# Five kept places for split weights from the output projection to the plain FFN tiles, and the down projection's group additions on VectorE

## The chip, the cores and the metric

One core of a Trainium2 chip runs one launch of the kernel. The metric is the device time of the launch in microseconds (us); the kernel before is given as the median of three runs. Engines: PE is TensorE, DVE is VectorE, ACT is ScalarE, POOL is GpSimd, SP is SyncE, whose queue issues the weight DMAs.

## The reference

One decoder layer of width 2048 on 512 tokens in float32: token mixing, cross-attention into 256 memory tokens, and a SwiGLU feed-forward of width 5632. The parts that matter here are the end of the cross-attention and the feed-forward:

```python
for l in range(DEPTH):
    ...
    y = memory_cross_attention(h, mem_n, w_xq[l], w_xkv[l], w_xo[l])   # ends in o @ wo, 512 x 2048
    x = x + rms_norm(y, ln_x_post[l])
    h = rms_norm(x, ln_ffn_pre[l])
    y = (jax.nn.silu(h @ w_gate[l]) * (h @ w_up[l])) @ w_down[l]
    x = x + rms_norm(y, ln_ffn_post[l])
```

## The kernel before

Every matrix product is done in three matmuls of a reduced-precision type: a float32 value is split into a high part, a cast on ScalarE (L96), and a low part, the difference, on VectorE (L97), and `mm3` (L112 to L114) issues high x high, high x low and low x high. A weight tile therefore costs a DMA into a raw buffer, a cast and a subtraction before TensorE can use it. The raw buffers are a ring of four (`wraw`), the parts a ring of three (`whi`, `wlo`). The 512 tokens stand in the columns and are worked in two halves of 256 (`HALVES`) from the cross-attention's output projection to the plain FFN tiles. The order of instructions on each engine is made by a scheduler from the dependences and the order of the program; `high_priority(AHEAD)` brings a weight's DMA, cast and subtraction forward.

The output projection `wo(j, t, stat)` runs over 8 weight tiles j of `w_xo` for half t = 0, then t = 1. `net.kept` puts the last three tiles of the first half at the front of the second half, since their parts still stand in the ring; the other five are loaded and split again. In the first half the last attention head is done between the tiles. Then come the inputs of the FFN, `ffn_input(k, t, stat)`, 16 tiles of each half: a DMA of the residual (L641), two VectorE operations (L643, L646), a DMA out (L647), a split (L99 on ScalarE, L100 on VectorE) and a square on ScalarE (L201), whose sums are taken by GpSimd (L203) and by small matmuls against a vector of ones (L213). The first half's inputs and `plain(0)`, the four plain tiles of the FFN (16 weight tiles of 512 KB of `w_gu`) follow; then the second half's inputs (`second()`) and `plain(1)`, which again begins with the three weight tiles that are kept.

The other 40 FFN tiles and most of the down projection are done by a Strassen scheme (`strassen`). For a group it loads 6 or 8 weight tiles of 256 KB, makes three combinations of each (L948 and L949 on VectorE, L950 on GpSimd), casts and subtracts 128x896 (L96, L97), and does 21 matmuls into PSUM banks psO, psG, psS, psT. At the end of a group ScalarE copies one bank and VectorE adds the results into `e` (L963 to L966). In the FFN `swiglu` follows, two VectorE operations of 128x512 (L877, L879) and a silu between them (L878). In the down projection there are two rounds s of 8 groups; after each group GpSimd adds `e` into two output tiles, 128x512 each, 32 additions in all:

```python
for k, o in ((j, 0), (j + hp, 5)):
    nc.gpsimd.tensor_tensor(ys[k], ys[k], e[:, o * 256:(o + 2) * 256], op=ALU.add)   # L1063
```

Of the kernel before, what the change touches and what calls it, by code (L numbers as in the profile page):

```python
# [33 lines left out]
class Net:  # L34
    def __init__(self, ctx, tc, a):
        self.tc, self.nc, self.a = tc, tc.nc, a
        nc = self.nc
        self.rings = {}
        self.const = ctx.enter_context(tc.tile_pool(name="const", bufs=1))
        self.wp = ctx.enter_context(tc.tile_pool(name="wp", bufs=1))  # L40
        self.tp = ctx.enter_context(tc.tile_pool(name="tp", bufs=2))
        self.ps = ctx.enter_context(tc.tile_pool(name="ps", bufs=1, space=PSUM))
        self.dr = ctx.enter_context(tc.tile_pool(name="dr", bufs=1, space=DRAM))
        c = self.const
        right = ctx.enter_context(tc.tile_pool(name="rpad", bufs=1, side="right"))
        nc.vector.memset(right.tile([P, 8], F32, name="rpad"), 0.0)
        self.gains = c.tile([P, len(GAINS), KD], F32, name="gains")
        nc.gpsimd.dma_start(self.gains, a["gains"])
        self.ident = c.tile([P, P], F32, name="ident")
        nc.gpsimd.dma_start(self.ident, a["c_ident"])  # L50
        self.ones = c.tile([P, P], F32, name="ones")
        nc.vector.memset(self.ones, -0.375)
        self.oneD = c.tile([P, 1], F32, name="oneD")
        nc.vector.memset(self.oneD, 1.0 / D)

    def ring(self, name, dtype, n):
        if name not in self.rings:
            self.rings[name] = [[self.wp.tile([P, 1024], dtype, name=f"{name}{i}") for i in range(n)], 0]
        r = self.rings[name]
        r[1] += 1  # L60
        return r[0][(r[1] - 1) % n]

    def kept(self, order):

        return [*order[-3:], *order[:-3]]

    def wtiles(self):
        return self.ring("wraw", F32, 4), self.ring("whi", FR, 3), self.ring("wlo", FR, 3)

# [32 lines left out]
    def weight(self, src, into=None):  # L102
        n = src.shape[1]
        raw, hi, lo = self.wtiles() if into is None else (self.ring("wraw", F32, 4), *into)
        with self.tc.high_priority(AHEAD):
# [544 lines left out]
def sublayer2(net, mctx, ms):  # L650
# [164 lines left out]

    held, last_j = {}, range(KD // 2)[-3:]

    def wo(j, t, stat):
        hi, lo = held[j] = held.pop(j) if t and j in last_j else net.weight(a["w_xo"][j])
        for jj in range(2):  # L820
# [15 lines left out]
    for j in range(KD // 2):  # L836
        if j in (0, 2, 4):
            next(last)
        wo(j, 0, st0)
    k3ctx.close()  # L840
    net.rstd(st0, rb[:, HALVES[0]])
    st1, stx = MeanSq(net, ka, nc.gpsimd, 256, "sy1"), MeanSq(net, ka, nc.gpsimd, 256, "sx0")
    for j in net.kept(range(KD // 2)):
        wo(j, 1, st1)
# [16 lines left out]

    return xctx, xs, x0, yctx, ys, rbf, rf, x2T, second, close

# [5 lines left out]

def ffn(net, xctx, xs, xt0, yctx, ys, rb, rf, x2T, second, close):  # L870
    tc, nc, a = net.tc, net.nc, net.a
# [12 lines left out]
    def plain(t):  # L884
# [5 lines left out]
        parts = [[q for q in order if q[1] == f] for f in range(NPLAIN)]  # L890
        for j, f in order:
            ps, first, last = banks[f], (j, f) == parts[f][0], (j, f) == parts[f][-1]
            if (j, f) in held:
                hi, lo = held.pop((j, f))
            else:
                u, hi, lo = [v.rearrange("p (j b c) -> p j b c", b=4, c=P) for v in net.wtiles()]
                with tc.high_priority(AHEAD):
                    nc.sync.dma_start(u, a["w_gu"][f, j:j + 2].rearrange("j p b c -> p j b c"))
                    net.split(hi, lo, u)
            if not t and (j, f) in order[-3:]:  # L900
                held[j, f] = hi, lo
# [143 lines left out]
    for s in range(2):  # L1045
# [11 lines left out]
        for j in range(hp):  # L1057
# [4 lines left out]
            for k, o in ((j, 0), (j + hp, 5)):  # L1062
                nc.gpsimd.tensor_tensor(ys[k], ys[k], e[:, o * 256:(o + 2) * 256], op=ALU.add)  # L1063
        late = net.last(nc.vector, nc.scalar)
# [230 lines left out]
```

## Time and profile before

| | us |
|---|---|
| median of three runs | 2799.49 (2798.63 to 2800.45) |
| the profiled execution | 2799.45 |
| its span | 2797.7 |
| TensorE busy in it | 2741.7 (98%) |
| VectorE busy | 2011.7 (72%) |
| ScalarE busy | 1252.1 (45%) |
| GpSimd busy | 612.8 (22%) |
| mean TensorE clock granted | 0.996 of full |

The profile comes from one execution. A row of a timeline gives the start within the span, the length, the engine, the source line of the kernel and the tiles written and read; in brackets stands how long the engine had been idle and what ended that. The length of an instruction overlaps a little with the next one's on its engine, so the distance from start to start is the shorter and better price. A row of waits gives the idle time of an engine by the instruction that it waited for. Matmuls of 128x256 follow each other at 0.12 us.

### The profile page before, as it was taken

To read this page: it belongs to the slowest core of one execution; us is meant where nothing else is said; L and a number is where in the kernel's file an instruction comes from. 1 tells how busy PE (TensorE), PEld (TensorE's weight loads), DVE (VectorE), ACT (ScalarE), POOL (GpSimd) and SP (SyncE) were. 2 spreads that over 40 slices of the span, in tenths; PEclk is the share of its full clock that TensorE was granted. 3 is DMA by queue.
4 is the path that set the end of the run, shared out by engine and by line. 5 is a ranking of instruction groups with operands and counts; after the bars stand their busy time and mean duration, and the time that the engine had idled before them with its cause. 6 is when DMAs were issued, how large, how long until landed. Compare 5 with 4: busy or idle time off the path is not lost.

```text
span 2797.7 us, 48879 instructions
## 1 busy us (share of the span) xinstructions
PE 2741.7 (98%) x18384; PEld 2517.8 (90%) x18384; DVE 2011.7 (72%) x3752; ACT 1252.1 (45%) x2061; POOL 612.8 (22%) x715
## 2 busy tenths in 40 slices
PE   9999999999999999999999999999999999999998
PEld 7788887888878889999989999999999999989996
DVE  5655656565645445777798888888988888899756
ACT  4333545454533235654764444444444444343353
POOL 0000000000000000010333444444224223525303
PEclk9999999999999999999999999999999999999999
DMA  6434332333336456763564444444444453444474
GB/s 186 117 101 131 99 96 78 97 97 109 96 105 200 146 154 213 240 214 121 166 203 128 121 118 120 119 121 120 122 115 125 117 170 105 119 136 106 150 247 165
DMA packets 168493, 384.16 MB, mean 137 GB/s; under 512 B 19312, under 2 KB 39840, under 8 KB 168128
## 3 DMA queue, kind: packets, MB, share of 16 engines
q1 hardware_dynamic: 158816, 352.39, 42.1%
q0 software_dynamic: 8864, 27.60, 3.0%
q8 instruction: 144, 2.36, 0.4%
q10 hardware_dynamic: 576, 1.05, 0.1%
q14 instruction: 93, 0.76, 0.1%
HBM read 343.32 MB, written 37.64 MB: 136 GB/s over the span
## 4 chain that ended last, share of the span: by engine, by line
PE 78%; DVE 12%; DMA 6%; issue 2%; ACT 1%; POOL 0%; DVEq 0%; SPq 0%; POOLq 0%; ACTq 0%
PE psG L112 15%; PE psG L114 15%; PE psG L113 15%; DVE wlo L97 5%; PE psS L112 4%; PE psS L113 4%; PE psS L114 4%; PE psT L112 3%; PE psT L114 3%; PE psT L113 3%; DMA wraw<-in_w_dst_dram 3%; DMA wraw<-in_w_gu_dram 2%; PE psO L114 2%; PE psO L112 2%; PE psO L113 2%
## 5 line engine op out<-in xcount | busy, mean ns | idle before, releaser
L96 ACT CAST whi<-wraw 128x896 fp32r<-128x896 f32 (+2 forms) x773 | 758.3, 984 | 1064.1 <-PE psT L114 340.8
L97 DVE TENSOR_TENSOR wlo<-wraw,whi 128x896 fp32r<-128x896 f32 (+2 forms) x773 | 907.4, 1175 | 263.8 <-ACT whi L96 261.0
L950 POOL TENSOR_TENSOR wraw<-wraw 128x128 f32<-128x128 f32 x416 | 415.6, 1001 | 676.1 <-DVE wraw L949 546.9
L112 PE MATMUL psG<-xh,whi 128*128 128x512 f32 (+1 forms) x1072 | 401.0, 374 | 1.6 <-ACT whi L96 1.5
L114 PE MATMUL psG<-xh,wlo 128*128 128x512 f32 (+1 forms) x1072 | 400.1, 373 | 0.8 <-DVE wlo L97 0.8
L113 PE MATMUL psG<-xl,whi 128*128 128x512 f32 (+1 forms) x1072 | 399.7, 373 | 0.0
L112 PEld LDWEIGHTS psG<-xh,whi 128*128 128x128 f32 x1072 | 203.1, 189 | 35.6 <-ACT whi L96 2.9
L114 PEld LDWEIGHTS psG<-xh,wlo 128*128 128x128 f32 x1072 | 202.4, 189 | 33.9 <-DVE wlo L97 1.0
L113 PEld LDWEIGHTS psG<-xl,whi 128*128 128x128 f32 x1072 | 202.8, 189 | 32.5
L948 DVE TENSOR_TENSOR wraw<-wraw 128x128 f32<-128x128 f32 x416 | 137.8, 331 | 103.2 <-DMA wraw<-in_w_gu_dram 67.3
L949 DVE TENSOR_TENSOR wraw<-wraw 128x256 f32<-128x256 f32 x416 | 185.6, 447 | 6.8
L112 PE MATMUL psT<-th,whi 128*128 128x256 f32 x640 | 179.4, 280 | 0.0
L113 PE MATMUL psT<-tl,whi 128*128 128x256 f32 x640 | 178.8, 279 | 0.0
L114 PE MATMUL psT<-th,wlo 128*128 128x256 f32 x640 | 178.7, 279 | 0.0
L114 PE MATMUL psG<-x,wlo 128*128 128x256 f32 (+1 forms) x544 | 158.1, 291 | 3.3 <-DVE wlo L97 3.3
L112 PE MATMUL psG<-x,whi 128*128 128x256 f32 (+1 forms) x544 | 156.8, 288 | 1.5 <-ACT z L764 1.5
L113 PE MATMUL psG<-x,whi 128*128 128x256 f32 (+1 forms) x544 | 157.5, 290 | 0.0
L112 PE MATMUL psG<-mh,whi 128*128 128x256 f32 x512 | 143.4, 281 | 1.1 <-ACT y L630 1.1
L113 PE MATMUL psG<-ml,whi 128*128 128x256 f32 x512 | 143.1, 280 | 0.0
L114 PE MATMUL psG<-mh,wlo 128*128 128x256 f32 x512 | 142.7, 281 | 0.0
L112 PE MATMUL psS<-xh,whi 128*128 128x256 f32 x480 | 134.8, 281 | 1.4 <-ACT xh L99 1.4
L113 PE MATMUL psS<-xl,whi 128*128 128x256 f32 x480 | 135.0, 282 | 0.9 <-DVE xl L100 0.9
(482 smaller groups left out, 7297.2 us busy)
## 6 DMA issues: line engine op xcount, KB each, us to landing
wraw<-in_w_gu_dram SPq DMA_DIRECT2D x320, 256.0 KB, 2.7
wraw<-in_w_z_dram SPq DMA_DIRECT2D x64, 512.0 KB, 3.8
wraw<-in_w_mix_dram SPq DMA_DIRECT2D x64, 512.0 KB, 4.5
wraw<-in_w_down_dram SPq DMA_DIRECT2D x61, 512.0 KB, 5.3
wraw<-in_w_dst_dram SPq DMA_DIRECT2D x96, 256.0 KB, 2.7
wraw<-in_w_gu_dram SPq DMA_DIRECT2D x29, 512.0 KB, 3.7
wraw<-in_w_qk_dram SPq DMA_DIRECT2D x24, 512.0 KB, 3.6
actT<-zs POOLq DMA_DIRECT2D x40, 256.0 KB, 2.3
```

The source lines that it names most:

```text
L96: nc.scalar.copy(hi, x)
L97: nc.vector.tensor_tensor(lo, x, hi.bitcast(F32), op=ALU.subtract)
L112: mm(ps, lh, rh, start=start, stop=False)
L113: mm(ps, lh, rl, start=False, stop=False)
L114: mm(ps, ll, rh, start=False, stop=stop)
L948: nc.vector.tensor_tensor(u[:, 4], u[:, 0], u[:, 3], op=ALU.add)
L949: nc.vector.tensor_tensor(u[:, 5:7], u[:, 0:5:4], u[:, 1:2].broadcast_to([P, 2, P]), op=ALU.subtract)
L950: nc.gpsimd.tensor_tensor(u[:, 7], u[:, 2], u[:, 6], op=ALU.subtract)
```

## The change

Two edits. The ring of parts gets two more places (`kh`, `kl`) for a time: they are made in the space of the pool `k3`, which holds the tiles of the attention heads, when that is closed after the fifth tile of the first half of `wo`, and taken out again at the middle of `plain(1)`. `kept` goes by the number of places that the ring has, so that `wo` and `plain` reuse five tiles in their second half, not three. And the two additions at the end of a down projection's group move from GpSimd to VectorE.

```diff
+    def more(self, slots):
+        self.parts[:0] = slots
+
+    def fewer(self, slots):
+        self.parts[:] = [s for s in self.parts if s not in slots]
 
     def kept(self, order):
-        return [*order[-3:], *order[:-3]]
+        n = len(self.parts)
+        return [*order[-n:], *order[:-n]]
...
-    held, last_j = {}, range(KD // 2)[-3:]
+    held = {}
 
     def wo(j, t, stat):
-        hi, lo = held[j] = held.pop(j) if t and j in last_j else net.weight(a["w_xo"][j])
+        if t and j in held:
+            hi, lo = held.pop(j)
+        else:
+            hi, lo = net.weight(a["w_xo"][j])
+            if not t:
+                held[j] = hi, lo
...
         wo(j, 0, st0)
-    k3ctx.close()
+        if j == 4:
+            k3ctx.close()
+            kw = k2ctx.enter_context(tc.tile_pool(name="kw", bufs=1, side="right"))
+            wide = net.slots(kw, FR, 2, "kh", "kl")
+            net.more(wide)
...
-    for j in net.kept(range(KD // 2)):
+    order = net.kept(range(KD // 2))
+    for j in order[len(net.parts):]:
+        held.pop(j)
+    for j in order:
         wo(j, 1, st1)
...
-        for j, f in order:
+        for i, (j, f) in enumerate(order):
+            if t and i == len(order) // 2:
+                net.fewer(wide)
...
-            if not t and (j, f) in order[-3:]:
+            if not t and (j, f) in order[-len(net.parts):]:
                 held[j, f] = hi, lo
...
             for k, o in ((j, 0), (j + hp, 5)):
-                nc.gpsimd.tensor_tensor(ys[k], ys[k], e[:, o * 256:(o + 2) * 256], op=ALU.add)
+                nc.vector.tensor_tensor(ys[k], ys[k], e[:, o * 256:(o + 2) * 256], op=ALU.add)
```

The rest of the diff gives the rings another form with the same places. The lines of the changed kernel are numbered 10 higher around the splits and 24 higher from the FFN on. In its order VectorE has 32 additions more and 4 splits less, ScalarE 4 casts less, GpSimd 32 additions less, SyncE 4 DMAs of 512 KB less (11 of `w_xo`, not 13; 27 of `w_gu`, not 29), and TensorE the same number of instructions.

VectorE at the end of a group of the down projection's first round, before (L965 and L966 are the last writes of `e`; the L97 behind them is the next group's second weight tile):

```order
L965 TENSOR_TENSOR e_23901<-psT_23736,e_23901 128x512
L966 TENSOR_TENSOR e_23901<-psT_23736,e_23901 128x256
L948 TENSOR_TENSOR wraw1_184<-wraw1_184 128x128
L97 TENSOR_TENSOR wlo0_190<-wraw3_186,whi0_187 128x896
L949 TENSOR_TENSOR wraw1_184<-wraw1_184 128x256
L948 TENSOR_TENSOR wraw2_185<-wraw2_185 128x128
L949 TENSOR_TENSOR wraw2_185<-wraw2_185 128x256
L97 TENSOR_TENSOR wlo1_191<-wraw0_183,whi1_188 128x896
```

The same place on VectorE in the changed kernel:

```order
L989 TENSOR_TENSOR e_23897<-psT_23732,e_23897 128x512
L990 TENSOR_TENSOR e_23897<-psT_23732,e_23897 128x256
L972 TENSOR_TENSOR wraw1_62<-wraw1_62 128x128
L1087 TENSOR_TENSOR y9_23198<-y9_23198,e_23897 128x512
L107 TENSOR_TENSOR wlo1_68<-wraw3_64,whi1_67 128x896
L1087 TENSOR_TENSOR y1_23190<-y1_23190,e_23897 128x512
L973 TENSOR_TENSOR wraw1_62<-wraw1_62 128x256
L972 TENSOR_TENSOR wraw2_63<-wraw2_63 128x128
L107 TENSOR_TENSOR wlo2_70<-wraw0_61,whi2_69 128x896
```

The additions stand one ahead of and one behind the next split; on GpSimd's side they are gone from between two L950.

ScalarE at the end of the FFN's second input half, before (`xh` is the high part of an input tile, `sq256` its square, `zs` the plain tiles' silu):

```order
L99 ACTIVATE xh7_10296<-y7_8041,gains_74 128x256
L201 ACTIVATE sq256_13295<-y7_8041 128x256
L878 ACT_TABLE_LOAD
L878 ACTIVATE zs_13129<-zs_13129 128x256
L878 ACTIVATE zs_13134<-zs_13134 128x256
L878 ACTIVATE zs_13139<-zs_13139 128x256
L878 ACTIVATE zs_13144<-zs_13144 128x256
L99 ACTIVATE xh15_10312<-y15_8049,gains_74 128x256
L201 ACTIVATE sq256_13304<-y15_8049 128x256
```

The same place on ScalarE in the changed kernel:

```order
L900 ACT_TABLE_LOAD
L900 ACTIVATE zs_13130<-zs_13130 128x256
L900 ACTIVATE zs_13135<-zs_13135 128x256
L109 ACTIVATE xh14_10310<-y14_8048,gains_84 128x256
L211 ACTIVATE sq256_13286<-y14_8048 128x256
L900 ACTIVATE zs_13140<-zs_13140 128x256
L109 ACTIVATE xh7_10296<-y7_8041,gains_84 128x256
L211 ACTIVATE sq256_13296<-y7_8041 128x256
L109 ACTIVATE xh15_10312<-y15_8049,gains_84 128x256
L211 ACTIVATE sq256_13305<-y15_8049 128x256
```

The table load and three silus have moved ahead of the last input tiles' casts and squares.

TensorE in the first half of `wo`, from the last attention matmul (psO) of the changed kernel to its first uses of the two new places:

```order
L124 MATMUL psO_11965<-xph_11973,xv11_10328 128x256
L122 MATMUL psG_11985<-xoh1_10979,whi0_65 128x256
L123 MATMUL psG_11985<-xol1_10983,whi0_65 128x256
L124 MATMUL psG_11985<-xoh1_10979,wlo0_66 128x256
L122 MATMUL psG_11985<-xoh2_10980,whi0_65 128x256
L123 MATMUL psG_11985<-xol2_10984,whi0_65 128x256
L124 MATMUL psG_11985<-xoh2_10980,wlo0_66 128x256
L122 MATMUL psG_11985<-xoh3_10981,whi0_65 128x256
L123 MATMUL psG_11985<-xol3_10985,whi0_65 128x256
L124 MATMUL psG_11985<-xoh3_10981,wlo0_66 128x256
L122 MATMUL psG_12030<-xoh0_10978,kh0_12023 128x256
L123 MATMUL psG_12030<-xol0_10982,kh0_12023 128x256
```

and at that place before, where the next tile stands in the second of the three places:

```order
L112 MATMUL psG_11985<-xoh3_10981,whi0_187 128x256
L113 MATMUL psG_11985<-xol3_10985,whi0_187 128x256
L114 MATMUL psG_11985<-xoh3_10981,wlo0_190 128x256
L112 MATMUL psS_12039<-xoh0_10978,whi1_188 128x256
L113 MATMUL psS_12039<-xol0_10982,whi1_188 128x256
```

The sixth tile's matmuls now read a place that comes free with the attention's tiles.

## Rows read from the trace of the kernel before

**Rows 1.** the page, part 1: busy time, share of the span, instructions

```profile
PE 2741.7 (98%) x18384; PEld 2517.8 (90%) x18384; DVE 2011.7 (72%) x3752; ACT 1252.1 (45%) x2061; POOL 612.8 (22%) x715
```

**Rows 2.** table by stretches: stretch, length, busy time by engine, clock, DMA share

```profile
1364.00:1404.00 40.00, 33.80 (x275) 32.57 (x274) 39.49 (x66) 29.08 (x64) 23.70 (x23) 1.00 0.71 221
1404.00:1444.00 40.00, 37.37 (x279) 35.96 (x280) 37.84 (x80) 23.21 (x46) 16.63 (x13) 0.94 0.76 243
...
1600.00:2200.00 600.00, 599.67 (x5048) 599.24 (x5047) 515.47 (x905) 251.56 (x302) 249.59 (x271) 1.00 0.42 120
2330.00:2645.00 315.00, 301.48 (x2276) 288.86 (x2276) 272.95 (x418) 123.50 (x153) 140.80 (x125) 1.00 0.42 117
```

**Rows 3.** TensorE's waits, 2330 to 2650: total us, times, longest

```profile
PE psO L114 <- DVE wlo L97: 13.4, 15, 1.7
```

**Rows 4.** timeline of VectorE, down projection's group boundary: start, length

```profile
2371.74 0.68 DVE L965 TENSOR_TENSOR e<-psT,e 128x512 f32<-128x512 f32 x1
...
2372.67 1.28 DVE L948 TENSOR_TENSOR wraw<-wraw 128x128 f32<-128x128 f32 x1
2373.88 2.17 DVE L97 TENSOR_TENSOR wlo<-wraw,whi 128x896 fp32r<-128x896 f32 x1
```

**Rows 5.** timelines of GpSimd, ScalarE, TensorE there; last, the longest wait

```profile
2372.50 2.60 POOL L1063 TENSOR_TENSOR y<-y,e 128x512 f32<-128x512 f32 x2 [0.35 <-DVE e L965]
...
2372.68 0.94 ACT L96 CAST whi<-wraw 128x896 fp32r<-128x896 f32 x1 [1.58 <-PE psT L114]
...
2376.11 0.38 PE L114 MATMUL psO<-xh,wlo 128*128 128x256 f32 x1 [0.72 <-DVE wlo L97]
...
2410.25 0.38 PE L114 MATMUL psO<-xh,wlo 128*128 128x256 f32 x1 [1.66 <-DVE wlo L97]
```

**Rows 6.** timeline of VectorE, a group boundary in the FFN

```profile
1818.60 0.28 DVE L948 TENSOR_TENSOR wraw<-wraw 128x128 f32<-128x128 f32 x1
1818.80 1.09 DVE L97 TENSOR_TENSOR wlo<-wraw,whi 128x896 fp32r<-128x896 f32 x1
1819.80 0.69 DVE L877 TENSOR_TENSOR zs<-e,rb 128x512 f32<-128x512 f32 x1
1820.40 0.42 DVE L949 TENSOR_TENSOR wraw<-wraw 128x256 f32<-128x256 f32 x1
```

**Rows 7.** VectorE by line: FFN (1600 to 2200), down projection (2330 to 2640)

```profile
L97 DVE TENSOR_TENSOR wlo<-wraw,whi 128x896 fp32r<-128x896 f32 x242 | 268.7, 1110 | 34.7 <-ACT whi L96 33.9
...
L948 DVE TENSOR_TENSOR wraw<-wraw 128x128 f32<-128x128 f32 x241 | 73.9, 306 | 45.4 <-DMA wraw<-in_w_gu_dram 44.2
...
L97 DVE TENSOR_TENSOR wlo<-wraw,whi 128x896 fp32r<-128x896 f32 x96 | 118.0, 1231 | 3.4 <-ACT whi L96 3.4
...
L948 DVE TENSOR_TENSOR wraw<-wraw 128x128 f32<-128x128 f32 x92 | 36.9, 401 | 33.1 <-DMA wraw<-in_w_dst_dram 32.8
```

**Rows 8.** TensorE's waits, 1364 to 1460

```profile
PE psG L114 <- DVE wlo L97: 5.2, 5, 2.0
...
PE psT L213 <- POOL sx L203: 0.9, 1, 0.9
```

**Rows 9.** VectorE by line and form, 1365 to 1443

```profile
L97 DVE TENSOR_TENSOR wlo<-wraw,whi 128x1024 fp32r<-128x1024 f32 x19 | 24.1, 1270 | 1.6 <-ACT whi L96 1.6
L646 DVE TENSOR_TENSOR y<-y,x 128x256 f32<-128x256 f32 x32 | 16.7, 530 | 1.9 <-DMA x<-x1T 1.9
```

**Rows 10.** timeline of ScalarE, end of the FFN input's second half

```profile
1442.03 1.28 ACT L878 ACT_TABLE_LOAD   x1
...
1444.96 0.40 ACT L201 ACTIVATE sq<-y 128x256 f32<-128x256 f32 x1
```

**Rows 11.** table by stretches of 2 us (columns as in rows 2)

```profile
1444.00:1446.00 2.00, 2.00 (x12) 2.00 (x11) 1.79 (x6) 2.00 (x7) 1.51 (x3) 0.50 0.21 72
```

**Rows 12.** timelines of ScalarE and VectorE, a w_xo tile's cast and split

```profile
1344.82 1.05 ACT L96 CAST whi<-wraw 128x1024 fp32r<-128x1024 f32 x1
...
1345.90 1.23 DVE L97 TENSOR_TENSOR wlo<-wraw,whi 128x1024 fp32r<-128x1024 f32 x1 [0.45 <-ACT whi L96]
```

More of the change, by code (lines that the diff above doesn't have):

```diff
@@ L37, in __init__ @@
         nc = self.nc
-        self.rings = {}
         self.const = ctx.enter_context(tc.tile_pool(name="const", bufs=1))
         self.wp = ctx.enter_context(tc.tile_pool(name="wp", bufs=1))
+        self.raws = self.slots(self.wp, F32, 4, "wraw")
+        self.parts = self.slots(self.wp, FR, 3, "whi", "wlo")
         self.tp = ctx.enter_context(tc.tile_pool(name="tp", bufs=2))
@@ L54, in __init__, with slots, turn @@
         nc.vector.memset(self.oneD, 1.0 / D)
[L56 to L61, printed above, removed]
+    def slots(self, pool, dtype, n, *names):
+        return [tuple(pool.tile([P, 1024], dtype, name=f"{name}{i}") for name in names) for i in range(n)]
+    @staticmethod
+    def turn(ring):
+        ring.append(ring.pop(0))
+        return ring[-1]
+    def more(self, slots):
+        self.parts[:0] = slots
+    def fewer(self, slots):
+        self.parts[:] = [s for s in self.parts if s not in slots]
     def kept(self, order):
-        return [*order[-3:], *order[:-3]]
+        n = len(self.parts)
+        return [*order[-n:], *order[:-n]]
     def wtiles(self):
-        return self.ring("wraw", F32, 4), self.ring("whi", FR, 3), self.ring("wlo", FR, 3)
+        return *self.turn(self.raws), *self.turn(self.parts)
     def psum(self, tag, shape=(P, 512)):
@@ L103, in weight @@
         n = src.shape[1]
-        raw, hi, lo = self.wtiles() if into is None else (self.ring("wraw", F32, 4), *into)
+        raw, hi, lo = self.wtiles() if into is None else (*self.turn(self.raws), *into)
         with self.tc.high_priority(AHEAD):
@@ L860, in close @@
         kctx.close()
-    return xctx, xs, x0, yctx, ys, rbf, rf, x2T, second, close
+    return xctx, xs, x0, yctx, ys, rbf, rf, x2T, second, close, wide
 NPLAIN = 4
@@ L867, with ffn @@
 SLICES = ((0, PL), (PL + NS, PL), (2 * PL + 2 * NS, NF - 2 * PL - 2 * NS))
-def ffn(net, xctx, xs, xt0, yctx, ys, rb, rf, x2T, second, close):
+def ffn(net, xctx, xs, xt0, yctx, ys, rb, rf, x2T, second, close, wide):
     tc, nc, a = net.tc, net.nc, net.a
```

## The prediction

> **What bounds the kernel now.** I read the busy line first: TensorE works 2741.7 of 2797.7 us [rows 1], so a change that removes no matmul can win at most the 56 us in which TensorE stands, plus what a lowered clock costs. The changed kernel has the same 18,294 TensorE instructions in its order as the kernel before. The table by stretches then says where it stands [rows 2]: the Strassen part of the FFN (1600 to 2200) is full, 599.67 of 600 us; the down projection (2330 to 2645) lacks 13.5 us; the second half of the cross-attention output projection with the FFN's inputs and the plain FFN tiles (1364 to 1444) lacks 6.2 and 2.6 us. The change touches just these two last places. TensorE's waits in the down projection are one row: 13.4 us in 15 waits, all for the low part of a split weight, written by VectorE, at a psO matmul [rows 3]. There is one such wait at nearly each of the 16 Strassen groups, where one group ends and the next begins.
>
> **Down projection, the mechanism.** At such a boundary VectorE finishes e (L965 at 2371.74), and GpSimd starts its two additions y += e at 2372.50 and runs 2.60 us [rows 4, 5]. VectorE's next two instructions lie beside them: the small addition L948 takes 1.28 us and the split L97 takes 2.17 us, from 2373.88 to 2376.05 [rows 4]. That split is the one TensorE waits for, from 2375.39 to 2376.11 [rows 5]. In the FFN the same function has the same boundary with no GpSimd addition, and there L948 takes 0.28 and L97 1.09 us [rows 6]. The pair loses 1.00 + 1.08 = 2.08 us at each boundary, while GpSimd adds. The means say so too: L948 306 ns in the FFN and 401 here, L97 1110 and 1231 [rows 7]; 92 x 0.095 + 96 x 0.121 = 20.4 us of VectorE time.
>
> **What the 32 additions cost on VectorE.** Their shape, 128x512 with both inputs in SBUF, is that of L877 in the FFN, at the same point after e: it starts at 1819.80 and the next instruction starts at 1820.40, so 0.60 us each [rows 6]. The rows of before hold 30 of them, 18.0 us, against 20.4 us that VectorE gets back: its load in this part does not grow (272.95 of 315 us now [rows 2]). The order of the changed kernel puts the first addition between L948 and the critical split, the second behind it. From 2372.67, the old start of L948: 0.20 for L948 (1818.60 to 1818.80 in the FFN), 0.60 for the addition, which is 2373.47; the split waits for its cast, 2372.68 + 0.94 = 2373.62 [rows 5], and takes 1.09 [rows 6]: 2374.71 instead of 2376.05. That is 1.34 us earlier. TensorE wanted it at 2375.39, so the wait is gone. The longest of the 15 is 1.66 us [rows 5]; the mean is 13.4 / 15 = 0.9. Only three are over 1.34, and they leave some 0.5 us together. What is late next is the following split: 2374.71, less 0.1 of overlap, plus 0.60 for the second addition, 0.3 for L949, 0.20 for L948 starts it near 2375.8, which is no later than the end of the critical split in the kernel before, so nothing new is late. I take **-12.5 us** for this edit. At best it is all 13.4; the other bound is the slower rival below.
>
> What I cost at nothing: GpSimd's subtractions L950, which stood behind the two additions in its queue, come sooner, if anything. The operands of the second Strassen part are ordered behind VectorE's last instruction, which is now the second addition, some 1.2 us later; the plain tiles' matmuls of that part lie over them. Without that cover it is 1.2 us, once.
>
> A rule speaks against this edit: the Trainium skill, "Perfetto Trace Analysis", section "Optimizing Scalar/DVE Operations", says that with a saturated VectorE it may make sense to move work to ScalarE or even to GpSimd, the opposite of what is done here; it adds that GpSimd and VectorE share a read port, so that a move between those two might not help. By the rule alone the 32 additions would be 19 us more on a VectorE that is 87% busy, the slower rival below; the caveat is what the 1.28 and 2.17 us of [rows 4] show, and there the trace agrees with it.
>
> **Five places, what it removes.** Two places more keep two more split tiles from one half of the tokens to the next, at the output projection and at the plain tiles: in the order there are 4 DMAs of 512 KB, 4 ScalarE casts and 4 VectorE splits less. VectorE is what counts: in 1364 to 1404 it is busy 39.49 of 40 us, in 1404 to 1444 37.84 [rows 2], and it does 19 splits at 1.27 us there [rows 9]. TensorE lacks 8.8 us in these two stretches, and its waits from 1364 to 1460 are for such low parts more than for anything else, 5.2 us [rows 8]. They can't all be won. TensorE's sums of squares (L213) stand in its queue between the first matmuls of the second half of the plain tiles, and the last needs the square of the last x, which needs VectorE's last L646. Until there a wait that goes away early only makes TensorE arrive earlier at the sums. So the gain is by how much the sums open earlier. Between the first L643 and that last L646 VectorE's order has 142 instructions before, 18 of them splits, and 141 now, 16 of them splits. Two splits, at some 1.15 us each (1.23 [rows 12], less a little overlap with the next instruction), are **2.3 us**. Then ScalarE: before, the last cast of x and its square stand behind a table load, from 1442.03, and four silus; the square runs 1444.96 to 1445.36 [rows 10]. In the new order the table load and two silus stand ahead of the pair of x14 and one more ahead of that of x7, so that they fall in time in which ScalarE waits for VectorE; up to 1.2 us. Together 3 to 3.5 us. The other sum of squares, of the first half, waited 0.9 us for GpSimd [rows 8]; the same backlog limits it.
>
> Against it stands a new wait. The two new places are cut from space that the attention's tiles held, so the cast of the sixth w_xo tile, which was done ahead, now comes after the last attention matmul, and TensorE reaches its first matmul with that tile nine matmuls later, 9 x 0.119 = 1.1 us (0.119 is 600 us by 5048 [rows 2]). Cast (1.05 us) and split (1.23 us) [rows 12] make 2.28 us. The order gives TensorE six matmuls that need only high parts, 0.7 us; the rest is 2.28 - 1.1 - 0.7 = 0.5, and with a y copy ahead of the cast about 0.7 us. Bounds: 0 and 1.5.
>
> The clock: in the stage it falls to half where TensorE has stood, 0.50 from 1444 to 1446 [rows 11], which is 1 us lost in that window. Waits that are only shorter may leave it so, and I count nothing for it. Sum of this edit: -3.3 + 0.7, taken as **-2.5 us**. Bounds: +1, if the sums open no earlier and the new wait is 1 us; -6.5, if most of the 8.8 us came back.
>
> **The sum.** 12.5 + 2.5 = 15.0 us off the profiled execution's 2799.45 us gives 2784.45; the median before is 2799.49, 0.04 above the profiled one, so 2784.5.
>
> **The rivals.**
> (a) *The five places give nothing.* VectorE's last x also waited 1.9 us for DMAs of x [rows 9]; if these don't come earlier, two splits less only make VectorE wait longer there, and the gain of ScalarE is eaten by the new wait. Then only the additions work: 2799.5 - 12.5 = 2787. For it: that DMA row. Against: four weight DMAs less on the same queue.
> (b) *The critical split comes only a third of a microsecond earlier.* GpSimd, free of the additions, does its L950 subtractions at once, and these may lie beside the same split: its L950 and VectorE's L97 would then hold each other as the additions did. 0.35 us at 15 boundaries, where two of the waits are shorter than that, is 5.0 us; with the 2.5 of the other edit 2792, without it 2794.5. For it: L950 also works on SBUF. Against: in the FFN, where L950 is free to run, L97 has a mean of 1110 ns, hardly over its 1.09 [rows 6, 7].
> (c) *Slower: VectorE is the bound, and the slow pair is not GpSimd's doing.* If the 1.28 and 2.17 us of [rows 4] stayed (the cause being DMA writes, say), each critical split would come 0.60 us later for the addition put ahead of it. 15 x 0.60 = 9.0 us, less 2.5: 2799.5 + 6.5 = 2806; without the 2.5, 2808.5. It decides if L948 beside the boundary keeps over 1 us. Against: the FFN boundary, with the same DMA share of 0.42 [rows 2], has 0.28 and 1.09.
> (d) *Nothing.* Halfway between (b) and (c), part of the slow pair stays and the addition uses up what is won: about 2798.
> (e) *The five places give more:* 6 us, since the clock also stays up: 2781.
>
> **How the numbers follow.** Chances: forecast 0.57 (2784.5, some 2782 to 2787), (a) 0.14, (b) 0.12, (e) 0.03, (d) 0.06, (c) 0.08. All of the first four are faster by more than 0.2% (5.6 us, about what a measurement of this kernel can tell from no change): 0.86. Within 0.2%: 0.06, from (d). Slower: 0.08, from (c). The range goes from 2799.5 - 13.4 - 6.5 = 2779.5 up into (b), to 2793.5, and leaves out (c), (d) and the tail of (b), less than 2 in 10.
>
> **What would show it.** In the changed kernel's trace the waits of TensorE in the down projection should fall from 13.4 to under 2 us; L948 beside the boundary should take about 0.3 and the critical split about 1.1 us, with two additions of about 0.68 us on VectorE at each boundary, and VectorE's busy time there should stay within a few us of 273. If those are right and the waits remain, the order around the split was wrong. In the earlier stage the last square of the FFN input should come some 3 us earlier relative to the start of the output projection's second half, and one wait of under 1.5 us should stand at the sixth w_xo tile. I am wrong if L948 and L97 stay long, or if the waits move to another matmul.

## The result, and the profile after

The changed kernel takes 2780.15 us (median of 4 runs, 2777.91 to 2782.07) against 2799.06 (4 runs, 2798.39 to 2800.45): ratio 0.9933, 95% interval 0.9917 to 0.9949. That is 18.9 us faster, inside the range of 2779.5 to 2793.5 and 4.4 us below the forecast of 2784.5. Measured once more beside other runs of the kernel before it was 2777.01 against 2795.07, again 0.9933 (0.9921 to 0.9945). Both kernels vary by 2 to 7 us from run to run, so comparisons below go by ratios.

The page's busy line and the stretch of the down projection (columns as in [rows 1, 2]; lines are numbered 10 to 24 higher now, L1087 is the addition, L107 the split, L972 and L973 the combinations):

```profile
PE 2738.3 (98%) x18384; PEld 2517.7 (91%) x18384; DVE 1996.5 (72%) x3780; ACT 1245.9 (45%) x2057; POOL 543.8 (20%) x683
...
2325.00:2630.00 305.00, 301.76 (x2296) 290.89 (x2295) 263.11 (x455) 123.83 (x155) 95.73 (x93) 1.00 0.43 123
```

VectorE, which took over 32 additions, is busy 15 us less, and GpSimd 69 us less. TensorE's waits in the down projection, which answer to [rows 3]:

```profile
PE psO L124 <- DVE wlo L107: 2.9, 5, 1.0
```

The same group boundary as in [rows 4, 5], VectorE:

```profile
2366.51 0.68 DVE L989 TENSOR_TENSOR e<-psT,e 128x512 f32<-128x512 f32 x1
...
2367.52 0.29 DVE L972 TENSOR_TENSOR wraw<-wraw 128x128 f32<-128x128 f32 x1
2367.73 0.69 DVE L1087 TENSOR_TENSOR y<-y,e 128x512 f32<-128x512 f32 x1
2368.33 1.09 DVE L107 TENSOR_TENSOR wlo<-wraw,whi 128x896 fp32r<-128x896 f32 x1
2369.34 0.69 DVE L1087 TENSOR_TENSOR y<-y,e 128x512 f32<-128x512 f32 x1
```

The pair that took 1.28 and 2.17 us is back to 0.29 and 1.09, the prices of the FFN's boundary [rows 6], with one addition between and one behind it. From the start of L972 to the end of the split it is 1.90 us; the prediction had 2.04, the kernel before 3.38. The means, which answer to [rows 7]:

```profile
L107 DVE TENSOR_TENSOR wlo<-wraw,whi 128x896 fp32r<-128x896 f32 x96 | 104.9, 1095 | 11.5 <-ACT whi L106 11.5
...
L972 DVE TENSOR_TENSOR wraw<-wraw 128x128 f32<-128x128 f32 x95 | 29.1, 306 | 23.9 <-DMA wraw<-in_w_dst_dram 23.7
L1087 DVE TENSOR_TENSOR y<-y,e 128x512 f32<-128x512 f32 x30 | 20.5, 697 | 0.0
```

L948 fell from 401 to 306 ns and L97 from 1231 to 1095, close to the FFN's 306 and 1110 [rows 7], and an addition takes 697 ns, 0.60 from start to start.

Where the time went, by the start of the same instruction in both traces (the first addition into e of a group, L963 and L987): at the first Strassen group of the FFN the changed kernel is 2.7 us ahead (1513.22 and 1510.54), at the last one 5.0 (2292.95 and 2287.99), at the last group of the down projection 17.3 (2640.35 and 2623.03), at the end of the span 17.4. So 12.4 us come in the down projection. The 2.3 us within the FFN are not the change's: in the traces of all twelve runs below, some of them with the same code there, the way from the first group's `e` to the fourth's is 2.4 to 4.5 us shorter than in this one execution of the kernel before.

The other place, ahead of the FFN's Strassen groups: TensorE's waits from 1364 to 1460, to hold against [rows 8], then the end of the FFN's second input half on ScalarE, against [rows 10], and TensorE at its first use of a new place:

```profile
PE psT L223 <- POOL sx L213: 3.3, 1, 3.3
PE psT L189 <- DVE zs L187: 0.8, 1, 0.8
PE psG L123 <- DVE x L110: 0.6, 1, 0.6
PE psS L124 <- DVE wlo L107: 0.3, 1, 0.3
```

```profile
1437.05 1.28 ACT L900 ACT_TABLE_LOAD   x1
...
1441.72 0.40 ACT L211 ACTIVATE sq<-y 128x256 f32<-128x256 f32 x1
...
1346.81 0.38 PE L122 MATMUL psS<-xoh,kh 128*128 128x256 f32 x1 [0.21 <-ACT kh L106]
```

The 5.2 us of waits for low parts of weights are down to 0.3; the wait at the first sums has grown from 0.9 to 3.3. The last square starts at 1441.72, 3.2 us earlier, and this execution was 0.9 us late when it came to the output projection (its first wait there ends at 1333.30, before at 1332.39), so the sums open 4.1 us earlier. The new wait is 0.2 us.

Of these 4.1 us only 2.7 + 0.9 = 3.6 are left at the first Strassen group. TensorE's granted clock can account for that. Stretches of both kernels around the waits (columns as in [rows 2], the clock is the third number from the end; first two of the kernel before, then two of the changed one):

```profile
1405.00:1409.00 4.00, 4.00 (x21) 3.82 (x21) 4.00 (x11) 1.82 (x4) 0.00 (x0) 0.57 0.87 269
1442.00:1447.00 5.00, 4.40 (x25) 4.26 (x25) 4.23 (x13) 4.97 (x13) 2.17 (x4) 0.66 0.35 120
...
1402.00:1413.00 11.00, 8.42 (x37) 8.15 (x38) 11.00 (x25) 4.71 (x10) 1.62 (x2) 0.53 0.88 287
1442.00:1447.00 5.00, 5.00 (x44) 5.00 (x45) 2.89 (x15) 5.00 (x14) 0.44 (x1) 1.00 0.27 87
```

In the kernel before the clock is lowered twice, after TensorE had waited 2.0 and 0.9 us (to 1400.09 and 1403.97) and 1.4 and 0.6 us (to 1441.75 and 1443.27); in the changed kernel once, around the 3.3 us wait that ends at 1403.77, but for longer: it is 0.50, the lower of its two levels (1.2 GHz), from 1403 to 1412. With TensorE's busy time times what the clock lacks, an estimate from these rows, that is 4.00 x 0.43 + 4.40 x 0.34 = 3.2 us before and 8.42 x 0.47 = 4.0 us now: 0.8 us more.

### The profile page after: what moved, and what is told of

The parts are those of the page before. It is cut to its first block, busy times and chain, and to the rows that moved or that the text cites. A ratio compares the mean times of both kernels' runs of the same rounds, so it can differ in the third digit from the quotient of the medians.

```text
span 2780.3 us, 48847 instructions
## 1 busy us (share of the span) xinstructions
PE 2738.3 (98%) x18384; PEld 2517.7 (91%) x18384; DVE 1996.5 (72%) x3780; ACT 1245.9 (45%) x2057; POOL 543.8 (20%) x683
## 4 chain that ended last, share of the span: by engine, by line
PE 87%; DVE 7%; DMA 3%; issue 1%; ACT 1%; POOL 0%; SPq 0%; DVEq 0%; ACTq 0%; POOLq 0%
PE psG L122 16%; PE psG L124 16%; PE psG L123 16%; PE psS L122 5%; PE psS L124 5%; PE psS L123 5%; PE psT L122 4%; PE psT L124 4%; PE psT L123 4%; DVE wlo L107 2%; PE psO L124 2%; PE psO L122 2%; PE psO L123 2%; PE psT L552 1%; DMA wraw<-in_w_dst_dram 1%
## 5 line engine op out<-in xcount | busy, mean ns | idle before, releaser
L106 ACT CAST whi<-wraw 128x896 fp32r<-128x896 f32 (+3 forms) x759 | 743.1, 983 | 1055.4 <-PE psG L123 343.1
L107 DVE TENSOR_TENSOR wlo<-wraw,whi 128x896 fp32r<-128x896 f32 (+3 forms) x759 | 877.1, 1157 | 274.6 <-ACT whi L106 271.6
L974 POOL TENSOR_TENSOR wraw<-wraw 128x128 f32<-128x128 f32 x416 | 397.0, 957 | 726.5 <-DVE wraw L973 602.8
L973 DVE TENSOR_TENSOR wraw<-wraw 128x256 f32<-128x256 f32 x416 | 185.3, 446 | 6.1
L972 DVE TENSOR_TENSOR wraw<-wraw 128x128 f32<-128x128 f32 x416 | 129.0, 310 | 78.4 <-DMA wraw<-in_w_gu_dram 52.0
L122 PE MATMUL psG<-x,whi 128*128 128x256 f32 (+1 forms) x512 | 148.0, 289 | 1.8 <-ACT z L774 1.8
L124 PE MATMUL psG<-x,wlo 128*128 128x256 f32 (+1 forms) x512 | 148.7, 290 | 0.1
L123 PE MATMUL psG<-x,whi 128*128 128x256 f32 (+1 forms) x512 | 148.4, 290 | 0.0
L107 DVE TENSOR_TENSOR ptl<-psT,pth 128x512 fp32r<-128x512 f32 x96 | 63.3, 687 | 101.3 <-ACT pth L106 101.1
L532 ACT ACTIVATE pr<-pr,mx 128x128 f32<-128x128 f32 (+7 forms) x192 | 90.4, 472 | 101.2 <-DVE mx L528 100.7
```

Of the source, the lines that this page charges most:

```text
L106: nc.scalar.copy(hi, x)
L107: nc.vector.tensor_tensor(lo, x, hi.bitcast(F32), op=ALU.subtract)
L122: mm(ps, lh, rh, start=start, stop=False)
L123: mm(ps, lh, rl, start=False, stop=False)
L124: mm(ps, ll, rh, start=False, stop=stop)
L532: nc.scalar.activation(o_, o_, AF.Exp, bias=mx[:, c:c + 1], scale=-1.0, accum_out=sm[:, c:c + 1])
```

## The experiments

The loss of TensorE in the table is not the idle time of the waits. It is taken from the starts of consecutive matmuls: what is over 0.12 us of each distance, summed over 280 us of the down projection, without the 128x512 matmuls of the plain tiles. Why this is larger is told below.

| kernel | median us | ratio to before (95%) | loss us | idle in psO waits us |
|---|---|---|---|---|
| before (profiled execution) | | 1 | 17.7 | 13.4 |
| changed, second measurement | 2777.01 | 0.9933 (0.9921 to 0.9945) | 3.5 | 1.5 |
| additions on VectorE alone | 2781.63 | 0.9945 (0.9931 to 0.9958) | 3.8 | 1.5 |
| five places alone | 2794.26 | 0.9993 (0.9984 to 1.0001) | 17.6 | 13.2 |
| no additions | 2777.42 | 0.9933 (0.9919 to 0.9946) | 0.6 | 0 |
| GpSimd memsets for additions | 2778.01 | 0.9935 (0.9922 to 0.9949) | 0.7 | 0 |
| GpSimd copies for additions | 2781.43 | 0.9948 (0.9934 to 0.9961) | 2.3 | 0.3 |
| GpSimd additions in quarters | 2787.86 | 0.9972 (0.9961 to 0.9984) | 9.7 | 4.3 |
| changed, additions twice | 2795.31 | 0.9998 (0.9988 to 1.0008) | 18.9 | 9.1 |
| changed, additions later | 2776.24 | 0.9934 (0.9920 to 0.9947) | 3.2 | 1.1 |
| changed, one sum of squares on VectorE | 2778.36 | 0.9937 (0.9925 to 0.9950) | 2.4 | 0.5 |

The first measurement's execution of the changed kernel lost 6.4 us by this count, the second's 3.5: the rest that remains varies.

**The two edits apart.** First only the additions, in the kernel before:

```diff
-                nc.gpsimd.tensor_tensor(ys[k], ys[k], e[:, o * 256:(o + 2) * 256], op=ALU.add)
+                nc.vector.tensor_tensor(ys[k], ys[k], e[:, o * 256:(o + 2) * 256], op=ALU.add)
```

> The kernel before with one edit: the 32 additions of the down projection on VectorE; three places as before. If the two edits are independent, this gives what the group ends of the down projection lost from before to after, 12.4 us (start of the last e: 17.3 us earlier, of it 4.9 before the down projection), so about 2786.5 us; L948 at the boundary about 0.3 us and the split about 1.1. Rival: the additions pay only together with the five places (the down projection starts with a better filled ring), then under 8 us, 2791 or more.

Then only the places: the changed kernel with that line the other way round.

> The changed kernel with the 32 additions back on GpSimd: five places alone. Independent edits: 5 to 6 us off, about 2793.5 to 2794.5, and 13 us of waits at psO in the down projection again. My forecast put this edit at 2.5 us, 2797; if that was right, what is over came from the additions, and this run gives 2796 to 2798.

The additions alone give 15.4 us (2796.44 x 0.0055; interval 11.7 to 19.3), the places alone 2.0 (interval from 4.5 faster to 0.3 slower). So my 12.4 for the additions was low, my 5 to 6 for the places did not come, and the 2.5 us of the forecast fits them. The two ratios multiply to 0.9938. The changed kernel was measured again to hold against that:

> The changed kernel itself, on the same chip and beside the same runs of the kernel before as the next ones. Additions alone gave a ratio of 0.9945 and places alone 0.9993; if the edits are independent this is 0.9938, some 17.3 us. Rival: they help each other (18.9 us was the first measurement, on other runs of the kernel before), then 0.993 or less.

It is 0.9933: the edits are independent as far as this can tell. The bigger part of what was over the forecast came from the additions, not from the places. With the places alone the slow rows are still there:

```profile
L107 DVE TENSOR_TENSOR wlo<-wraw,whi 128x896 fp32r<-128x896 f32 x94 | 115.7, 1232 | 3.4 <-ACT whi L106 3.4
...
L972 DVE TENSOR_TENSOR wraw<-wraw 128x128 f32<-128x128 f32 x91 | 38.8, 426 | 30.8 <-DMA wraw<-in_w_dst_dram 30.5
```

**What the additions cost at all.** The kernel before without them:

```diff
-                nc.gpsimd.tensor_tensor(ys[k], ys[k], e[:, o * 256:(o + 2) * 256], op=ALU.add)
+                pass
```

> The kernel before with the 32 additions left out altogether, on any engine. All theories: the psO waits of the down projection nearly gone, 12.5 to 13.5 us faster, 2786 to 2787. The distance from the run with the additions on VectorE is what they cost there: 0 to 1 us by my reckoning (VectorE has room); 2.5 us or more would mean that they are on the path.

It takes 2777.42 us, 19 less than the kernel before and some 9 below the 2786 to 2787 that I expected, though the waits that the additions caused were booked with 13.4 us of idle time. So GpSimd's additions cost more than their waits' rows say, and on VectorE they still cost 2781.63 - 2777.42 = 4.2 us. That is above the 0 to 1 us that I had reckoned.

The difference between row and loss is to be seen around one wait of the kernel before. The rows of the matmul ahead of the one in [rows 5] (2376.11, idle 0.72) and of the one behind it:

```profile
2375.11 0.28 PE L113 MATMUL psO<-xl,whi 128*128 128x256 f32 x1
...
2376.33 0.28 PE L112 MATMUL psG<-xh,whi 128*128 128x256 f32 x1
```

From 2375.11 to 2376.11 are 1.00 us where 0.12 would do, a loss of 0.88; the row gives 0.72, since it counts idle time from the end of the row ahead, which is 0.28 long, while the matmuls follow each other at 0.12. The next one starts 0.22 later, another 0.10. So a wait that the row gives as 0.72 cost 0.98. With 0.26 more for each of 15 waits, 13.4 become 17.3; the count gives 17.7, with some short waits that have no row at all.

**What in GpSimd's additions held VectorE.** In the kernel before, other GpSimd instructions of the same shape at the same place. A memset, which reads nothing (the additions are left out):

```diff
-                nc.gpsimd.tensor_tensor(ys[k], ys[k], e[:, o * 256:(o + 2) * 256], op=ALU.add)
+                nc.gpsimd.memset(e[:, o * 256:(o + 2) * 256], 0.0)
```

> The kernel before with each of the 32 GpSimd additions replaced by a GpSimd memset of the same 128x512 piece of e: GpSimd stands at the same place of its queue and writes as many bytes, but reads nothing; the additions are left out of the result. If GpSimd holds VectorE by any SBUF instruction, L948 and L97 at the boundary stay long by about the memsets' own length and most of the 13.4 us of waits stays: 2796 to 2800. If it needs GpSimd's reads, L948 is 0.28 and L97 1.09 there and the waits go: about 2787. If neither, and the waits came from L950 standing behind the additions in GpSimd's queue, L948 and L97 are short and the waits stay.

A copy, which reads one piece:

```diff
+                nc.gpsimd.tensor_copy(ys[k], e[:, o * 256:(o + 2) * 256])
```

> The kernel before with each of the 32 GpSimd additions replaced by a GpSimd copy of the same 128x512 piece of e into the output tile: one read in place of two; the additions are left out of the result. A memset there left VectorE alone (psO waits gone, L948 312 and L97 1102 ns on average). If any GpSimd read holds VectorE's two-input instructions, L948 at the boundary is again near 1 us, its mean 340 to 400 ns, and part of the 17 us stays, in proportion to the copies' length: 2785 to 2792. If it takes two reads, this equals the memset run, 2778.

The boundary with memsets, GpSimd and then VectorE:

```profile
2367.83 0.99 POOL L1063 MEMSET e<- 128x512 f32 x2 [0.34 <-DVE e L965]
...
2368.02 0.28 DVE L948 TENSOR_TENSOR wraw<-wraw 128x128 f32<-128x128 f32 x1
2368.38 1.09 DVE L97 TENSOR_TENSOR wlo<-wraw,whi 128x896 fp32r<-128x896 f32 x1
```

and with copies:

```profile
2367.86 1.23 POOL L1063 COPY y<-e 128x512 f32<-128x512 f32 x2 [0.35 <-DVE e L965]
...
2368.04 0.57 DVE L948 TENSOR_TENSOR wraw<-wraw 128x128 f32<-128x128 f32 x1
2368.53 1.49 DVE L97 TENSOR_TENSOR wlo<-wraw,whi 128x896 fp32r<-128x896 f32 x1
```

Both pairs of GpSimd instructions lie over L948 and the first part of L97, and the copies are hardly longer than the memsets (0.65 and 0.53 us each). Beside the memsets L948 and L97 take 0.28 and 1.09 us, as if alone. Beside the copies they take 0.57 and 1.49, together 0.69 more; the copies run 1.23 us. Beside the additions it was 2.08 more, and these ran 2.60 [rows 4, 5]. So a GpSimd instruction that reads SBUF holds a VectorE instruction with two SBUF inputs for much of its length, and one that only writes does not. The queue theory falls: with memsets the L950 stand behind something too, and no wait is left; and with the quarters of the next experiment, which hold GpSimd's queue for longer than the whole additions did (3.88 us for 2.60), the loss is smaller. My time for the copies, 2785 to 2792, was missed by 3.6 us: I had taken the loss in proportion, and of a third of the holding (0.69 of 2.08) only 2.3 us of 17.7 reached TensorE; L948 there was 0.57 us and not near 1. The Trainium skill, "SBUF — State Buffer", section "SBUF: two separate sides", says that VectorE and GpSimd share one pair of ports as an exclusive lock for a whole instruction, and that a VectorE instruction with two SBUF inputs is held only against a GpSimd instruction that reads SBUF. The rows agree, 0.28 beside a memset and 0.57 beside a copy.

**Smaller pieces on GpSimd.** The kernel before with each addition in four of 128x128:

```diff
+                for q in range(4):
+                    nc.gpsimd.tensor_tensor(ys[k][:, q * P:(q + 1) * P], ys[k][:, q * P:(q + 1) * P],
+                                            e[:, o * 256 + q * P:o * 256 + (q + 1) * P], op=ALU.add)
```

> The kernel before with each GpSimd addition cut into four of 128x128, same engine, same work. If GpSimd holds VectorE's two-input instructions for the rest of its own instruction and no longer, VectorE waits at most for one short piece (some 0.45 us) at a time: the critical split is still held, but by less, and the loss of 17 us falls to between 5 and 12 us. If VectorE is held whenever GpSimd has work of this kind, nothing is won: 2795.

```profile
2367.53 3.88 POOL L1064 TENSOR_TENSOR y<-y,e 128x128 f32<-128x128 f32 x6 [0.36 <-DVE e L965]
...
2367.71 0.43 DVE L948 TENSOR_TENSOR wraw<-wraw 128x128 f32<-128x128 f32 x1
2368.07 1.35 DVE L97 TENSOR_TENSOR wlo<-wraw,whi 128x896 fp32r<-128x896 f32 x1
2369.34 0.68 DVE L949 TENSOR_TENSOR wraw<-wraw 128x256 f32<-128x256 f32 x1
```

It gives 7.9 us (ratio 0.9972), and the loss of 9.7 is within the expected 5 to 12. The short additions, six of the group's eight in this row, let VectorE in between: L948 and L97 take 0.43 and 1.35, but the next one is held too (L949 0.68, against 0.42 in [rows 6]). The holding is per instruction; cutting it spreads the price and lets the critical split off with less.

**How much room VectorE has.** The changed kernel with every addition done twice:

```diff
                 nc.vector.tensor_tensor(ys[k], ys[k], e[:, o * 256:(o + 2) * 256], op=ALU.add)
+                nc.vector.tensor_tensor(ys[k], ys[k], e[:, o * 256:(o + 2) * 256], op=ALU.add)
```

> The changed kernel with each of the 32 VectorE additions done twice (so the result adds e twice): 32 x 0.6 = 19 us more work on VectorE in the down projection, where it is 86% busy. This measures how far off the slower rival was. If VectorE has the room that the sum assumed, up to 5 us slower than the changed kernel (2778 to 2782); if each addition at the boundary is on TensorE's path, 15 x 1.2 = 18 us slower, 2795.

It takes 2795.31, all 18 us lost again: by the ratios (0.9998 and 0.9933) 32 more additions cost 0.57 us each, their whole price. TensorE's waits from 2300 to 2645:

```profile
PE psO L122 <- ACT whi L106: 6.0, 5, 2.2
PE psO L124 <- DVE wlo L107: 3.1, 4, 1.4
PE psG L124 <- DVE wlo L107: 2.0, 2, 1.2
```

The waits are now also for high parts (ScalarE's cast). I had expected up to 5 us and had given the rival 18; the rival's number came. (One thing is mixed in: at most boundaries the scheduler put the first additions behind the critical split here.) The longest wait shows a way of paying that neither the sum nor the rival had in it. VectorE, GpSimd and ScalarE ahead of it, then all of ScalarE's waits for GpSimd's combination in 2330 to 2640, here and (last line, 2330 to 2620) in the kernel without additions:

```profile
2387.35 1.08 DVE L107 TENSOR_TENSOR wlo<-wraw,whi 128x896 fp32r<-128x896 f32 x1
2388.36 0.68 DVE L1088 TENSOR_TENSOR y<-y,e 128x512 f32<-128x512 f32 x1
...
2391.10 0.28 DVE L972 TENSOR_TENSOR wraw<-wraw 128x128 f32<-128x128 f32 x1
...
2387.37 4.33 POOL L974 TENSOR_TENSOR wraw<-wraw 128x128 f32<-128x128 f32 x1 [3.96 <-DVE wraw L973]
...
2391.73 0.94 ACT L106 CAST whi<-wraw 128x896 fp32r<-128x896 f32 x1 [7.34 <-POOL wraw L974]
...
ACT whi L106 <- POOL wraw L974: 93.1, 37, 7.3
...
ACT whi L96 <- POOL wraw L950: 10.5, 6, 2.2
```

From 2387.35 to 2391.38 VectorE goes from one instruction with two SBUF inputs to the next without a gap, and GpSimd's subtraction of 128x128, which takes 0.45 us at the shortest in this run, takes 4.33 and ends 0.3 us behind them. The cast waits for it, and TensorE for the cast. So the holding works the other way round too: additions on VectorE are paid for also by GpSimd's part of the next weight tile. The first 32 additions were cheaper on VectorE because GpSimd gave back what it had held; the next 32 cost their whole price.

**Is the rest the place of the first addition?** The changed kernel with both additions ordered behind two more splits of the next group:

```diff
+            if owing and j == 4:
+                owing()
...
+            def owing(j=j, e=e):
+                with net.behind(net.last(nc.vector)):
+                    for k, o in ((j, 0), (j + hp, 5)):
+                        nc.vector.tensor_tensor(ys[k], ys[k], e[:, o * 256:(o + 2) * 256], op=ALU.add)
```

> The changed kernel with both additions of a group held back on VectorE until two more splits of the next group are done. Counted as start-to-start distances of matmuls beyond 0.12 us, TensorE still loses 6.4 us in the down projection of the changed kernel, 0.6 without any additions. If the rest comes from the addition that stands ahead of the first split, it goes: 3 to 5 us faster than the changed kernel. Rival: it comes from VectorE's load as a whole, then within 1 us of it; or the second split becomes the late one, then slower.

Ratio 0.9934 against 0.9933, loss 3.2 against 3.5: my 3 to 5 us did not come. Between these two places of the additions no difference shows at this resolution. What sets the rest of their price stays open. It may be GpSimd's combination again: ScalarE's casts wait 64.9 us in 32 waits for it in the second execution of the changed kernel, 10.5 in 6 without additions; no run tests it.

**The same idea at another place.** The changed kernel with the running sum of squares of the first FFN input half on VectorE:

```diff
-    ... MeanSq(net, ka, nc.gpsimd, 256, "sx0")
+    ... MeanSq(net, ka, nc.vector, 256, "sx0")
```

> The changed kernel with 13 more additions taken from GpSimd: the running sum of squares of the first half of the FFN input (128x256 each), which TensorE waited for, 3.3 us at 1403.8. If the mechanism of the down projection holds here too, VectorE gets back about what they cost (13 x 0.33 = 4.3 us; beside GpSimd's additions its 128x2 instructions take 0.69 in place of 0.16 us), the sums open some 3 us earlier and the clock stays up: 2 to 5 us faster. Rival: VectorE is full here (37.8 of 40 us), the additions lengthen its queue: 1 to 4 us slower.

TensorE's waits from 1360 to 1470:

```profile
PE psS L122 <- ACT xh L109: 2.3, 2, 1.8
PE psS L123 <- DVE xl L110: 1.5, 2, 1.0
PE psT L223 <- POOL sy L213: 0.9, 1, 0.9
```

The wait of 3.3 us at the first sums is gone, and 2.3, 1.5 and 0.9 us stand in other places, at the end of the second input half (1430 to 1445). The time is the same (0.9937), and the first group's `e` starts at 1510.42, where the changed kernel has 1510.3 on average: the 2 to 5 us that I expected did not come. That VectorE is too full in this stage to gain by it is argued, not shown.

**The two uses of the places.** The changed kernel with the two places taken out after the output projection, and with them put in only there. The first:

```diff
     net.rstd(st1, rb[:, HALVES[1]])
+    net.fewer(wide)
     for k in PAIRED:
         ffn_input(k, 0, stx)
```

> The changed kernel with the two more places taken out after the output projection: 11 weight DMAs of the projection as in the changed kernel, 29 of the plain FFN tiles as before. Read by the start of the first Strassen group's e, which is within 0.3 us from run to run: 1513.1 to 1513.4 without the places, 1509.5 to 1510.5 with them. If VectorE's backlog up to the last FFN input makes the gain, as I worked out, the two splits saved here (all of the output projection) are ahead of it but also ahead of the first sums; 1511 to 1513.

The second:

```diff
             wide = net.slots(kw, FR, 2, "kh", "kl")
-            net.more(wide)
...
     net.rstd(st1, rb[:, HALVES[1]])
+    net.more(wide)
```

> The changed kernel with the two more places put in after the output projection: 13 weight DMAs of it as before, 27 of the plain FFN tiles. Its two splits less stand just between the last FFN inputs, in the backlog that sets the sums: 1510 to 1511 for the start of the first group's e, most of the 3 us. If it is near 1513, the gain comes from the output projection.

The first group's e starts at 1512.16 and at 1513.44. In the six other executions without the places it starts between 1512.07 and 1513.38 (mean 1513.0), in the six with both between 1509.51 and 1511.04 (mean 1510.3). So the two uses together bring 2.7 us, and neither alone can be told from nothing. My expectation for the plain tiles, 1510 to 1511, was wrong. TensorE's waits for the low parts and at the first sums, 1340 to 1470, first kernel and then the second:

```profile
PE psG L124 <- DVE wlo L107: 4.8, 3, 2.3
...
PE psT L189 <- DVE zs L187: 1.2, 1, 1.2
...
PE psG L124 <- DVE wlo L107: 3.8, 1, 3.8
PE psT L223 <- POOL sx L213: 3.1, 1, 3.1
```

Each alone leaves a long wait for a low part, 4.8 us in three and one of 3.8; with both these are gone. The clock adds to it: the first has three lowered stretches (0.60 in 1385 to 1389, 0.57 in 1399 to 1403, 0.66 in 1443 to 1448, with TensorE busy 4.00, 4.00 and 4.47 us), the second two (0.50 in 1379 to 1382 and in 1407 to 1416, busy 3.00 and 8.94 us). By the estimate used above that is 4.8 and 6.0 us, against 4.0 with both. In full time the two kernels (0.9944 and 0.9949, two runs each) can't be told from the changed one.

## Why the prediction was right, point by point

**The mechanism of the additions: right.** GpSimd's additions held the pair L948 and L97 (at ten of the 16 boundaries, with 1.26 to 1.28 and 2.15 to 2.18 us, and not at each; at most of the others they held other VectorE instructions); the prices 0.28, 1.09 and 0.60 that I took from the FFN's boundary came out as 0.29, 1.09 and 0.60. The memset, copy and quarter runs show that it is the reading and not the queue. Of the signs that I had named, L948, L97 and the additions came as said; the waits fell to 2.9 us and not under 2 in the first execution, and to 1.5 in the second.

**Their size: low, 12.5 us for a measured 15.4 (11.7 to 19.3).** The step that was off is the first: I took 13.4 us of idle time in [rows 3] as all that the waits cost. By the starts of the matmuls they cost 17.7. Against that stands some 4 us that the additions cost on VectorE where I took 0.5 to 0.9; the two errors have opposite signs, and that the sum came out near is in part luck. In the profiled executions the changed kernel wins 12.4 us in the down projection, since that one execution still lost 6.4.

**"Nothing new is late": not quite.** The five waits of 2.9 us that stayed are not those over 1.34 us of which I had counted 0.5, and four of them stand at other matmuls than the kernel before waited at. The two longest (0.97 and 0.84 us) are for the split two tiles earlier, just ahead of a group's first addition into `e`, and VectorE itself had stood idle there for that tile's DMA. VectorE and TensorE at the longest:

```profile
2592.27 0.29 DVE L972 TENSOR_TENSOR wraw<-wraw 128x128 f32<-128x128 f32 x1 [2.29 <-DMA wraw<-in_w_dst_dram]
...
2594.08 0.39 PE L124 MATMUL psO<-xh,wlo 128*128 128x256 f32 x1 [0.97 <-DVE wlo L107]
```

That the waits move to another matmul I had named as a sign of being wrong; four of the five did. Without additions on any engine there is no wait at all, so it is the additions' doing; the steps between are not shown.

**"VectorE's load does not grow": right, and all hung on it.** From the last FFN group's `e` to the last one of the down projection VectorE is busy 302.7 us in the kernel before and 289.0 with the additions alone on it:

```profile
2292.95:2640.35 347.40, 333.88 (x2402) 314.93 (x2401) 302.68 (x467) 146.68 (x189) 144.89 (x127) 1.00 0.43 122
2289.43:2621.43 332.00, 330.49 (x2402) 314.28 (x2401) 289.00 (x498) 145.99 (x189) 104.02 (x97) 1.00 0.43 127
```

That is 13.7 us less with 30 additions of 0.60 us more, so some 30 us came back where I had set 20.4 against 18.0. The slower rival's price of 0.6 us for each addition was right (the doubled additions: 0.57); only its condition was not met. VectorE had far less room than "272.95 of 315" sounds.

**The five places: near, 2.5 us for a measured 2.0 (from 4.5 faster to 0.3 slower).** Its terms: the sums opened 4.1 us earlier, for which I had 3 to 3.5; the new wait took 0.2 us, for which I had 0.7; the clock, for which I had nothing, took some 0.8. That removed waits only bring TensorE earlier to the sums was right: the wait at the first sums grew to 3.3 us. That the two uses pay only together I had not seen; the waits and the clock of the two runs show where it goes, and no run tells why. Whether the places bring anything in the full time is not shown by the measured times alone; the traces show 2.7 us at the first Strassen group, with no overlap between the six executions with them and the six without.

**The rule weighed against the change.** The Trainium skill, "Perfetto Trace Analysis", section "Optimizing Scalar/DVE Operations", says that work may be moved off a saturated VectorE, even to GpSimd, and adds that the two share a read port, so that a move between them might not help. Priced by rows of this case, the first half of that would have made the edit cost 19 us (32 x 0.6). The trace differs from it: the doubled additions cost that (18 us), those moved from GpSimd did not, since GpSimd had held VectorE for as long. It agrees with the second half (1.28 and 2.17 us beside GpSimd's additions, 0.29 and 1.09 without).

## What to carry to other kernels

Before work is given to GpSimd beside a busy VectorE, look at the lengths of VectorE's instructions that lie beside it: if an instruction with two SBUF inputs is longer there than elsewhere, the work may be cheaper on VectorE itself, and the sum is the time held against the price of the operation. Then look at GpSimd's other instructions, which VectorE held here in the same way. Count what a short wait of TensorE costs from the starts of the matmuls around it, not from the idle time of the row, which here left out 0.26 us of each.

## What was not expected of the hardware

A GpSimd memset of 128x512 (0.53 us on average) left VectorE's instructions alone, a copy of the same piece (0.65 us median) held them for 0.69 us in two. And GpSimd is held as well: its subtraction L950 of 128x128 takes 0.46 us at the shortest (2370.50 in the run with copies) and 1.19 us when it starts beside a running split (2371.38 there). With the additions done twice one took 4.33 us, beside seven VectorE instructions without a gap.
